# Narrower weights, skipped state products and a new order table in a gated-DeltaNet layer

## The chip, the cores and the metric

The kernel runs on one core of a Trainium2 chip. The metric is device time in microseconds (us). Before the change three runs gave 2718.79, 2718.13 and 2719.34 us, median 2718.79. All operands are float32; a matmul's operands can also be declared float32r, which the kernel uses for its large products by splitting every float into a high and a low part and adding three products.

## The reference, cut to what matters

One decoder layer (`DEPTH` is 1, so only layer 0) on 2048 tokens of width 1024. Its token mixer has eight gated-DeltaNet heads of width 128 and four heads that attend to a memory of 256 rows; their outputs go through one output projection, then a residual layer norm, an MLP with squared ReLU of width 4096, and a second layer norm. The part that the change touches is the chunked delta rule, with chunks of 64 rows in the reference:

```python
lower = jnp.where(strict, jnp.einsum('bnhcd,bnhsd->bnhcs', k_beta, kc) * decay, 0.0)
a_mat = jnp.eye(CHUNK, dtype=f32) + lower
u = lax.linalg.triangular_solve(a_mat, v_beta, left_side=True, lower=True, unit_diagonal=True)
w = lax.linalg.triangular_solve(a_mat, k_beta * jnp.exp(gc)[..., None], ...)
...
def step(state, inp):
    qd, kd, u_c, w_c, a_c, dc = inp
    v_new = u_c - jnp.einsum('bhcd,bhde->bhce', w_c, state)
    o = jnp.einsum('bhcd,bhde->bhce', qd, state) + jnp.einsum('bhcs,bhse->bhce', a_c, v_new)
    state = state * dc[..., None, None] + jnp.einsum('bhcd,bhce->bhde', kd, v_new)
    return state, o
s0 = jnp.zeros((B, H, Dk, v.shape[-1]), f32)
```

The first step starts from a zero state, and the state after the last step is not an output.

## The kernel before

**Tiling.** The tokens are taken in four blocks of 512 (`TB`), two blocks to a pair (`s` = 0, 1). In a block each head has four chunks of 128 rows (`NC`). A pair runs `mixer` for its two blocks (line 1655), then the output projection `out_seven` (line 1703), then `ff1` (1355) and `ff2` (1477). The last three are two-by-two block products that need seven block products instead of eight; in the profile their outputs are `ao`, `fA`, `fB`, `fC` and `f2A`, `f2B`, `f2C`. In `mixer` a step `t` runs `gdn_b` for head t-2, `gdn_a` for head t-1 and the projections of head t (`aq`, `ak`, `av`, and `az` for the gate), so that three heads are in work at once, and memory attention (`amq`, `sps`, `pmT`, `pmo`) stands between them.

**The inverse.** `invert` (line 889) inverts the unit lower triangular matrix of a head's four chunks. VectorE solves blocks of 16 rows; TensorE then doubles their size three times, each time by two products: `pq` (the off-diagonal block times the inverse so far) and `pp` (the inverse so far times `pq`). From 16 to 32 rows the weights are `LB` and `XB`, the latter with 112 columns. From 32 to 64 rows they are `L32` and `X32`, 128 columns wide, the two 32-row blocks of two chunks on the diagonal and 32 columns streamed through them (in the profile `pq<-Lq,inv` and `pp<-inv` with 128x32). From 64 to 128 rows they are `LP` and `X64` (`pq<-YP,inv` and `pp<-inv` with 128x64). Each `pq` and `pp` is two matmuls in float32, and there are 32 inversions (four blocks of eight heads). The tiles that hold these weights are zeroed once in a pair by `inverse_tiles` (line 551).

**The scan.** `gdn_b` (line 1074) walks the four chunks of a head: `pc<-state` and `po<-state` multiply k and the decayed q with the state, VectorE makes `R` from the first of them, `pc<-R,Y` applies the inverse, ScalarE copies the result to `vt`, `pc<-vt,kd` gives the state's increment, `po<-vt,at` completes the chunk's output, and VectorE updates the state. It does so for all 16 chunks, the first (zero state) and the last (state not read again) included. GpSimd sets the eight states to zero at the start (line 540).

**The end.** In `ff2` the last of the seven products adds, for eight groups of 512 rows of the weights (u = 0 to 7), into four banks, one for each tile of 128 tokens. Groups 0 to 4 go through the four tiles in turn. For the last three (`LT = 3`, line 1540) the order is turned round: tile 0 takes groups 5, 6 and 7, then tile 1, and so on, so that the tiles finish one after the other and each is normalized (`norm2`, DVE and GpSimd) and stored while TensorE does the next.

**What sets the order.** Each operation is first recorded (`Recorder.add`, line 225), with a cost by `cost` (line 277). `issue` (line 320) then runs a list scheduler over all of them: an operation becomes ready when its inputs' modelled ends are reached, plus a latency between the engines and `MARGIN` (100 ns, line 35), and of the ready ones each engine takes the one with the lowest priority number, which is its place in the program plus a shift from the table `PLACE` (line 190; keys such as `(0, 3, 'D')` name block, step and phase). The modelled starts give the order of every engine's instructions; on the chip each engine runs its own list in that order and waits where an operand is missing. All instructions are emitted at line 431, so a line number tells nothing; the names of the outputs do.

Of the kernel before, what the change touches and what calls it, by code (L numbers as in the profile page):

```python
# [11 lines left out]
ALU = mybir.AluOpType  # L12
# [22 lines left out]
MARGIN, TURN = 100, 40  # L35
# [149 lines left out]
class Op:  # L185
# [23 lines left out]
class Recorder:  # L209
# [110 lines left out]
    def issue(self):  # L320
# [50 lines left out]
        while True:  # L371
# [36 lines left out]
            for s in o.succ:  # L408
                lat = LAT.get((e, s.eng), LAT_FROM[e])
                if e == "PE" and lat and o.last < 60:  # L410
                    lat += 65 if o.last > 30 else 130
                if lat:
                    lat += MARGIN + (s.load if s.eng == "PE" and s.lhs in o.bufs else 0)
                s.ready = max(s.ready, o.end + (TURN if s.i in o.turns else lat))
                s.npred -= 1
                if s.npred == 0:
                    pending.append(s)
            for b in o.bufs:
                b.users -= 1
                b.end = max(b.end, o.end)  # L420
                if b.users == 0:
                    heapq.heappush(slots[b.key], b.end + LAT_FROM[e] + MARGIN)
                    again(b.key)
# [24 lines left out]
def hybrid_layer(  # L448
# [91 lines left out]
    for h in range(H):  # L540
        nc.gpsimd.memset(state[h], 0.0)
# [6 lines left out]
    INV = (("XB", (2, P)), ("LB", (2, P)), ("L32", (2, P)), ("X32", (2, P)), ("X64", (2, P)),  # L548
           ("LP", (2, P)), ("Q", (2 * P,)))

    def inverse_tiles():
        d = {}
        for i in range(0, len(INV), 2):
            t = slot("inv", "iv")
            nc.gpsimd.memset(t, 0.0)
            for j, (n, shape) in enumerate(INV[i:i + 2]):
                v = t[:, j * 2 * P:(j + 1) * 2 * P]
                d[n] = v if len(shape) == 1 else v.rearrange("p (u f) -> p u f", u=2)
        return d
# [184 lines left out]
    def gates(b, a):  # L744
# [46 lines left out]
        gc = G["gc"] = small("gc", sh, 2)  # L791
        gcf = gc.rearrange("p h c -> p (h c)")
        nc.vector.tensor_copy(gcf, pg[:, 0:32])
        G["ngc"] = small("ngc", sh, 2)
        nc.vector.tensor_scalar_mul(G["ngc"], gc, -1.0)
        kd = small("gkd", sh, 1)
# [15 lines left out]
        nc.tensor.transpose(pt[:32, :P], gcf, ident)  # L812
# [20 lines left out]
    def dense(b, h, T, G, w0=None):  # L833
# [29 lines left out]
        for n, nm in enumerate("kq"):  # L863
            pt = bank("pt" + nm, par)
            for c in range(NC):
                nc.tensor.transpose(pt[:, c * P:(c + 1) * P], res[nm][:, c * P:(c + 1) * P], ident)
            for c in range(NC):
                j = small("j" + nm, [P, P], 1)
                nc.scalar.activation(j, pt[:, c * P:(c + 1) * P], AF.Square,
                                     accum_out=ss[:, n * NC + c:n * NC + c + 1])  # L870
            if nm == "k":
                for c in range(NC):
                    nc.scalar.activation(kd[:, c * P:(c + 1) * P], pt[:, c * P:(c + 1) * P], AF.Copy,
                                         scale=G["ekd"][:, h, c:c + 1])
# [14 lines left out]
    def invert(L, par):  # L889
# [8 lines left out]
        for p in range(2):  # L898
            rows = slice(64 * p + 32, 64 * p + 64)
            nc.gpsimd.tensor_copy(L32[rows, :, 64 * p:64 * p + 32].part((0, p)), L[rows, 0:2, 64 * p:64 * p + 32])  # L900
            nc.vector.tensor_copy(L32[64 * p:64 * p + 32, :, 64 * p + 32:64 * p + 64].part((1, p)),
# [28 lines left out]
        XB, LB, X32, X64, Q = (inv[n] for n in ("XB", "LB", "X32", "X64", "Q"))  # L930
# [13 lines left out]
        Q16 = Q[:, :64].rearrange("p (u f) -> p u f", u=2)  # L944
# [4 lines left out]
        for c in range(2):  # L949
            nc.tensor.matmul(pp[:, c * 32:(c + 1) * 32], XB[:, c, :W], Q[:, c * 32:(c + 1) * 32].part(0, 3),  # L950
                             start=True, stop=True)
# [4 lines left out]
        ZP = Lq.rearrange("p c f -> p (c f)")[:, :64].rearrange("p (c f) -> p c f", c=2)  # L956
        Z = small("Z32", [P, NC, 32], 2)
        for p in range(2):
            odd = slice(64 * p + 32, 64 * p + 64)
            nc.vector.tensor_copy(ZP[64 * p:64 * p + 32].part(2 * p + 1), ZT[odd, 2:4])  # L960
            nc.scalar.copy(out=ZP[odd].part(2 * p), in_=ZT[odd, 0:2])
        nc.vector.transpose(Z.rearrange("p c f -> p (c f)"), ZT.rearrange("p c f -> p (c f)"))
        for p in range(2):
            for u in range(2):
                q = quads[2 * p + u]
                nc.vector.tensor_copy(X32[q, :, q].part((u, p)), Z[64 * p:64 * p + 32, 2 * u:2 * u + 2])
# [11 lines left out]
        pb = bank("pp", "ga%d" % par)[:, :64]  # L978
        pp = pb.rearrange("p (c f) -> p c f", c=2)
        for c in range(2):  # L980
            nc.tensor.matmul(pp[:, c], X32[:, c], Q[:, 64 + c * 32:64 + (c + 1) * 32].part(1), start=True, stop=True)
        Nf = Lq.rearrange("p c f -> p (c f)")[:, 64:]
        nc.scalar.activation(Nf, pb, AF.Copy, scale=-1.0)
        tr = Lq.rearrange("p c f -> p (c f)")[:64, :64]
        nc.vector.transpose(tr, Nf[:64])
        N3 = Nf.rearrange("p (c f) -> p c f", c=2)
        for p in (1, 0):
            o = Y3[64 * p:64 * p + 32, :, 64 * p + 32:64 * p + 64]
            nc.vector.tensor_copy(o[:, 2:4], N3[quads[2 * p + 1]])
            nc.scalar.copy(out=o[:, 0:2], in_=N3[quads[2 * p]])  # L990
        tr = tr.rearrange("p (c f) -> p c f", c=2)
        for u in range(2):
            nc.vector.tensor_copy(X64[quads[2 * u + 1], :, quads[2 * u]].part((u, 2)), tr[quads[u]])
# [7 lines left out]
        nc.scalar.copy(out=Q[:, P:].rearrange("p (c f) -> p c f", c=2).part(2), in_=pq)  # L1001
        pp = bank("pp", "ga%d" % par)[:, :P].rearrange("p (c f) -> p c f", c=2)
        for c in range(2):
            nc.tensor.matmul(pp[:, c], X64[:, c], Q[:, P + c * 64:P + (c + 1) * 64].part(2), start=True, stop=True)
# [12 lines left out]
    def gdn_a(h, r, G):  # L1017
# [50 lines left out]
        nc.scalar.activation(qd, gb, AF.Exp)  # L1068
        nc.vector.tensor_tensor(out=qd, in0=qd, in1=q, op=ALU.mult)
# [4 lines left out]
    def gdn_b(h, A, G, z, cat):  # L1074
# [5 lines left out]
        for c in range(NC):  # L1080
            pc = bank("pc", "pb")
            nc.tensor.matmul(pc[:, 0:P], k3[:, c], Sh, start=True, stop=True)
            nc.tensor.matmul(po[:, c], qd3[:, c], Sh, start=True, stop=False)
            R = small("R", [P, P], 2)
            nc.vector.scalar_tensor_tensor(out=R, in0=pc[:, 0:P], scalar=nbe[:, c:c + 1], in1=vb3[:, c],
                                           op0=ALU.mult, op1=ALU.add)
# [3 lines left out]
            nc.tensor.matmul(pc[:, 2 * P:3 * P], kd3[:, c], vt, start=True, stop=True)  # L1090
            nc.tensor.matmul(po[:, c], at3[:, c], vt, start=False, stop=True)
            nc.vector.scalar_tensor_tensor(out=Sh, in0=Sh, scalar=sc("el", c), in1=pc[:, 2 * P:3 * P],
                                           op0=ALU.mult, op1=ALU.add)
# [383 lines left out]
    def ff2(s, x1d):  # L1477
# [58 lines left out]
        for n, (xn, wn, bn, on, (th, nh)) in enumerate(SEVEN):  # L1536
# [3 lines left out]
            LT = 3 if last else 0  # L1540
# [114 lines left out]
    def mixer(b, T, w0, G):  # L1655
        i = b % 2
        r, A, z = {}, {}, {}
        for t in range(H + 2):
            spot(b, t, "B")
            if t >= 2:  # L1660
                c = cat_tile()
                gdn_b(t - 2, A.pop(t - 2), G, z.pop(t - 2), c[0])
                deliver(i, t - 2, *c)
            spot(b, t, "A")
            if 1 <= t <= H:
                A[t - 1] = gdn_a(t - 1, r.pop(t - 1), G)
# [250 lines left out]
```

## Time and profile before

| | |
|---|---|
| median of three runs | 2718.79 us |
| span of the profiled execution, first to last instruction | 2718.7 us |
| the profiled execution's own time | its span, which is 0.1 us from the median |
| TensorE (PE) busy, records | 2702.6 us (99%), 13625 |
| VectorE (DVE) busy | 2097.3 us (77%) |
| ScalarE (ACT) busy | 1627.0 us (60%) |
| GpSimd (POOL) busy | 403.6 us (15%) |
| mean granted TensorE clock | 0.999 |

In the views a group of instructions reads: line, engine, operation, output<-inputs, shape, count, then busy time of the group and mean duration of one, then the engine's idle time before them and what ended it. `128*112 128x32` at a matmul is weights of 128 rows and 112 columns with 32 columns streamed. A float32 matmul leaves two records, so 128 products of the scan leave 256; a transpose and a float32r matmul leave one. The ends of matmul records are modelled and overlap the next one's start, so what a matmul costs TensorE is read from the distance between starts, not from its duration. PEld is the weight load, which has a record of its own.

### The profile page before, as it was taken

To read this page: it belongs to the slowest core of one execution; us is meant where nothing else is said; L and a number is where in the kernel's file an instruction comes from. 1 tells how busy PE (TensorE), PEld (TensorE's weight loads), DVE (VectorE), ACT (ScalarE), POOL (GpSimd) and SP (SyncE) were. 2 spreads that over 40 slices of the span, in tenths; PEclk is the share of its full clock that TensorE was granted. 3 is DMA by queue.
4 is the path that set the end of the run, shared out by engine and by line. 5 is a ranking of instruction groups with operands and counts; after the bars stand their busy time and mean duration, and the time that the engine had idled before them with its cause. 6 is when DMAs were issued, how large, how long until landed. Compare 5 with 4: busy or idle time off the path is not lost.

```text
span 2718.7 us, 42521 instructions
## 1 busy us (share of the span) xinstructions
PE 2702.6 (99%) x13625; PEld 2264.0 (83%) x13625; DVE 2097.3 (77%) x5652; ACT 1627.0 (60%) x4106; POOL 403.6 (15%) x1031
## 2 busy tenths in 40 slices
PE   9999999999999999999999999999999999999998
PEld 7888888888888888888888888888888888888887
DVE  7999989998877776755767888788878666567575
ACT  7778767776575555334446776677656655554342
POOL 4233223331000000000022231332201000000000
PEclk9999999999999999999999999999999999999999
DMA  8766649867788888766663445444678644486673
GB/s 315 253 232 210 213 170 321 293 240 261 278 315 286 297 294 298 264 212 197 231 226 136 171 137 186 156 152 157 226 260 295 220 164 141 158 283 221 214 238 112
DMA packets 209072, 613.81 MB, mean 226 GB/s; under 512 B 24112, under 2 KB 32720, under 8 KB 188880
## 3 DMA queue, kind: packets, MB, share of 16 engines
q1 hardware_dynamic: 208416, 611.04, 64.7%
q8 instruction: 108, 1.77, 0.3%
q14 instruction: 116, 0.95, 0.1%
q10 hardware_dynamic: 432, 0.05, 0.0%
HBM read 436.35 MB, written 174.65 MB: 225 GB/s over the span
## 4 chain that ended last, share of the span: by engine, by line
PE 94%; DVE 2%; ACT 2%; DMA 1%; POOL 1%; issue 0%; SPq 0%; DVEq 0%; ACTq 0%; POOLq 0%
PE f2A L431 13%; PE fA L431 13%; PE ao L431 8%; PE fC L431 6%; PE f2C L431 6%; PE az L431 6%; PE aq L431 6%; PE av L431 6%; PE ak L431 6%; PE amq L431 3%; PE fB L431 3%; PE f2B L431 3%; PE pc L431 3%; PE po L431 2%; PE pkq L431 2%; PE pq L431 1%
## 5 line engine op out<-in xcount | busy, mean ns | idle before, releaser
L431 DVE TENSOR_TENSOR whl<-wraw,whl 128x512 fp32r<-128x512 f32 (+2 forms) x294 | 256.5, 883 | 109.8 <-ACT whl L431 107.9
L431 ACT CAST whl<-wraw 128x512 fp32r<-128x512 f32 (+2 forms) x294 | 226.4, 781 | 164.4 <-PE fC L431 54.5
L431 PE MATMUL fA<-B,whl 128*128 128x512 f32 x1152 | 279.1, 389 | 0.0
L431 PE MATMUL f2A<-whl,X 128*128 128x512 f32 x1152 | 262.1, 389 | 0.0
L431 ACT CAST X<-X 128x1024 fp32r<-128x1024 f32 x118 | 124.0, 1052 | 223.3 <-DMA X<-xsc 183.3
L431 PEld LDWEIGHTS fA<-B,whl 128*128 128x128 f32 x1152 | 216.2, 188 | 45.1
L431 PEld LDWEIGHTS f2A<-whl,X 128*128 128x128 f32 x1152 | 216.2, 188 | 44.9
L431 DVE TENSOR_TENSOR X<-X,X 128x1024 fp32r<-128x1024 f32 x118 | 143.8, 1221 | 126.0 <-ACT X L431 125.9
L431 PE MATMUL az<-T,whl 128*128 128x512 f32 x768 | 218.5, 406 | 0.0
L431 PE MATMUL aq<-T,whl 128*128 128x512 f32 x768 | 215.6, 406 | 1.7 <-DVE whl L431 0.8
L431 PE MATMUL ak<-T,whl 128*128 128x512 f32 x768 | 214.8, 407 | 0.1
L431 PE MATMUL av<-T,whl 128*128 128x512 f32 x768 | 209.1, 402 | 0.0
L431 PE MATMUL fC<-B,whl 128*128 128x512 f32 x768 | 192.3, 389 | 0.0
L431 PE MATMUL f2C<-whl,X 128*128 128x512 f32 x768 | 174.7, 389 | 0.0
L431 PEld LDWEIGHTS fC<-B,whl 128*128 128x128 f32 x768 | 144.1, 188 | 30.0
L431 PEld LDWEIGHTS f2C<-whl,X 128*128 128x128 f32 x768 | 144.1, 188 | 29.9
L431 PEld LDWEIGHTS aq<-T,whl 128*128 128x128 f32 x768 | 137.5, 189 | 27.4 <-DVE T L431 2.0
L431 PEld LDWEIGHTS av<-T,whl 128*128 128x128 f32 x768 | 138.5, 189 | 24.3
L431 PEld LDWEIGHTS ak<-T,whl 128*128 128x128 f32 x768 | 135.8, 189 | 22.3 <-ACT whl L431 0.4
L431 PEld LDWEIGHTS az<-T,whl 128*128 128x128 f32 x768 | 136.4, 189 | 21.2
L431 POOL TENSOR_SCALAR ve<-mv 128x1 f32<-128x1 f32 x34 | 15.3, 451 | 912.2 <-DVE mv L431 906.0
L431 PE MATMUL ao<-whl,X 128*128 128x512 f32 x528 | 136.8, 401 | 0.0
(294 smaller groups left out, 6292.2 us busy)
## 6 DMA issues: line engine op xcount, KB each, us to landing
whl<-wsc SPq DMA_DIRECT2D x108, 1024.0 KB, 4.9
wraw<-in_w_ff_dram SPq DMA_DIRECT2D x106, 512.0 KB, 4.3
X<-xsc SPq DMA_DIRECT2D x96, 512.0 KB, 4.1
wsc<-whl SPq DMA_DIRECT2D x36, 1024.0 KB, 6.4
whl<-tsc SPq DMA_DIRECT2D x64, 512.0 KB, 4.8
xsc<-hB SPq DMA_DIRECT2D x96, 256.0 KB, 2.5
xo<-cat SPq DMA_DIRECT2D x80, 256.0 KB, 4.1
wraw<-in_w_in_dram SPq DMA_DIRECT2D x35, 512.0 KB, 6.5
```

The source lines that it names most:

```text
L431: o.fn(*[res(a) for a in o.args], **{k: res(v) for k, v in o.kw.items()})
```

## The change

**Weights of 72 columns.** `L32` and `X32` become 72 columns wide (`W64`); the blocks of the two row pairs now stand side by side in 64 columns, and the streamed operands `Z64` and `Q64`, zero outside their blocks, are 64 columns wide for each of the two matmuls. So the pairs are `72x64` where they were `128x32`. ScalarE now copies `pq` with two copies of 64 partitions (before one of 128), and one transpose of 32 rows, one VectorE copy and one ScalarE copy stand where a transpose of 64 rows and two copies on each engine stood. The zeroed tiles are divided anew, still four.

**No products with the zero state.** In block 0 the first chunk has neither `pc<-state` nor `po<-state`; the inverse is applied to `vb` directly (`pc<-vb,Y`), and the state is copied from the increment. In block 3 the last chunk has no `pc<-vt,kd` and no update. The eight memsets of the states, a quarter of `qd` in block 0 and a quarter of `kd` in block 3 go too.

**Four last row groups by token tile.** `LT` is 4 in the last pair, so groups 4 to 7 of the last product go tile by tile.

**Slack behind GpSimd, and the order table.** `MARGIN` is now by engine, 400 ns behind GpSimd and 100 behind the others. `PLACE` has about twice as many entries, nearly all of them new. Beside these, the transpose `pgt` of the gates takes 96 columns in place of 32, of which 32 are used as before.

```diff
-MARGIN, TURN = 100, 40
+MARGIN, TURN = {"PE": 100, "DVE": 100, "ACT": 100, "POOL": 400, "SP": 100}, 40
...
-    ('w',): 140, (0, 0, 'H'): -305, (0, 1, 'D'): -225, (0, 1, 'H'): -435, (0, 1, 'Y'): -145, (0, 1, 'Z'): -165,
+    ('w',): 140, (0, 0, 'D'): 5, (0, 0, 'F'): -5, (0, 0, 'H'): -585, (0, 1, 'D'): -70, (0, 1, 'F'): 75,
...
-    for h in range(H):
-        nc.gpsimd.memset(state[h], 0.0)
...
-    INV = (("XB", (2, P)), ("LB", (2, P)), ("L32", (2, P)), ("X32", (2, P)), ("X64", (2, P)),
-           ("LP", (2, P)), ("Q", (2 * P,)))
+    W64 = 72
+    INV = ((("XB", (2, P)), ("LB", (2, P))), (("X64", (2, P)), ("LP", (2, P))),
+           (("L32", (2, W64)), ("X32", (2, W64)), ("Z64", (2, 64))),
+           (("Q64", (2, 64)), ("Q16", (64,)), ("N", (NC, 32)), ("Q", (P,))))
...
-        nc.tensor.transpose(pt[:32, :P], gcf, ident)
+        nc.tensor.transpose(pt[:96, :P], g3.rearrange("p j h c -> p (j h c)"), ident)
...
-        pq = bank("pq", "ga%d" % par)[:, :64].rearrange("p (c f) -> p c f", c=2)
+        pq = bank("pq", "ga%d" % par)[:W64, :P].rearrange("p (c f) -> p c f", c=2)
         for c in range(2):
             nc.tensor.matmul(pq[:, c], L32[:, c], ZP[:, c].part(0, 1, 2, 3), start=True, stop=True)
-        nc.scalar.copy(out=Q[:, 64:P].rearrange("p (c f) -> p c f", c=2).part(1), in_=pq)
...
+        for u in range(2):
+            nc.scalar.copy(out=QP[64 * u:64 * u + 64, :, 32 * u:32 * u + 32].part(u), in_=pq[:64, :, 32 * u:32 * u + 32])
+        pp = bank("pp", "ga%d" % par)[:W64, :P]
         for c in range(2):
-            nc.tensor.matmul(pp[:, c], X32[:, c], Q[:, 64 + c * 32:64 + (c + 1) * 32].part(1), start=True, stop=True)
...
+            nc.tensor.matmul(pp[:, c * 64:(c + 1) * 64], X32[:, c], QP[:, c].part(0, 1), start=True, stop=True)
...
+            begun, more = b > 0 or c > 0, b < NB - 1 or c < NC - 1
+            R = vb3[:, c]
+            if begun:
+                nc.tensor.matmul(pc[:, 0:P], k3[:, c], Sh, start=True, stop=True)
+                nc.tensor.matmul(po[:, c], qd3[:, c], Sh, start=True, stop=False)
...
+            if more:
+                nc.tensor.matmul(pc[:, 2 * P:3 * P], kd3[:, c], vt, start=True, stop=True)
+            nc.tensor.matmul(po[:, c], at3[:, c], vt, start=not begun, stop=True)
...
-            LT = 3 if last else 0
+            LT = (4 if 2 * s + 2 >= NB else 3) if last else 0
```

Three places show how the instructions move. The first is TensorE at the first inversion of block 0, the step from 32 to 64 rows; `az` and `amk` are products of the gate and of the memory's keys that fill the time between. Before:

```order
L431 MATMUL pp<-inv 112x32 x2
L431 MATMUL az<-T_192,whl 128x512
L431 MATMUL az<-T_218,whl 128x512
L431 MATMUL az<-T_225,whl 128x512
L431 MATMUL az<-T_218,whl 128x512 x2
L431 MATMUL az<-T_225,whl 128x512
L431 MATMUL pq<-Lq,inv 128x32 x2
L431 MATMUL az<-T_218,whl 128x512
L431 MATMUL az<-T_233,whl 128x512
L431 MATMUL az<-T_238,whl 128x512
L431 MATMUL az<-T_233,whl 128x512 x2
L431 MATMUL pp<-inv 128x32 x2
```

And after the change:

```order
L447 MATMUL pp<-inv 112x32 x2
L447 MATMUL av<-T_217,whl 128x512
L447 MATMUL amk<-mT,whl 128x256 x16
L447 MATMUL pq<-inv 72x64 x2
L447 MATMUL amk<-mT,whl 128x256 x8
L447 MATMUL az<-T_157,whl 128x512
L447 MATMUL az<-T_162,whl 128x512
L447 MATMUL az<-T_157,whl 128x512
L447 MATMUL pp<-inv 72x64 x2
```

The two pairs have 72 columns of weights and 64 streamed ones, and between them stand eight matmuls of 256 columns and three of 512 where five of 512 stood.

The second place is TensorE in block 0, where head 0's scan began beside the transposes of the memory rows (`pt<-ident,ym`). Before:

```order
L431 MATMUL pt<-ident,ym 128x128 x2
L431 MATMUL ptq<-ident,cq 128x128 x4
L431 MATMUL pt<-ident,ym 128x128 x8
L431 MATMUL pc<-state,ck 128x128
L431 MATMUL pt<-ident,ym 128x128 x4
L431 MATMUL aq<-T_171,whl 128x512
```

And after:

```order
L447 MATMUL az<-T_217,whl 128x512
L447 MATMUL pt<-ident,ym 128x128 x4
L447 MATMUL ptq<-ident,cq 128x128 x4
L447 MATMUL pt<-ident,ym 128x128 x12
L447 MATMUL aq<-T_157,whl 128x512
```

The product with the zero state is gone, and the last twelve transposes of the memory rows now follow each other.

The third place is VectorE at the kernel's end, from the third token tile's normalization on (`f2A` is the last product's bank, `mv` and `rs` the mean and the reciprocal deviation, `l2kq` the gain and the bias). Before:

```order
L431 BN_AGGR mv<-bn 128x2
L431 SCALAR_TENSOR_TENSOR y<-y,mv,l2kq_27882 128x512
L431 SCALAR_TENSOR_TENSOR y<-y,f2A 128x512
L431 SCALAR_TENSOR_TENSOR y<-y,mv,l2kq_27882 128x512
L431 BN_STATS bn<-y 128x6
L431 SCALAR_TENSOR_TENSOR y<-y,rs,l2kq_27917 128x512
L431 BN_AGGR mv<-bn 128x2
L431 SCALAR_TENSOR_TENSOR y<-y,rs,l2kq_27917 128x512
L431 SCALAR_TENSOR_TENSOR y<-y,mv,l2kq_27882 128x512 x2
L431 SCALAR_TENSOR_TENSOR y<-y,rs,l2kq_27917 128x512 x2
```

And after:

```order
L447 BN_AGGR mv<-bn 128x2
L447 SCALAR_TENSOR_TENSOR y<-y,mv,l2kq_27778 128x512 x2
L447 SCALAR_TENSOR_TENSOR y<-y,rs,l2kq_27813 128x512 x2
L447 SCALAR_TENSOR_TENSOR y<-y,f2A 128x512
L447 BN_STATS bn<-y 128x6
L447 BN_AGGR mv<-bn 128x2
L447 SCALAR_TENSOR_TENSOR y<-y,mv,l2kq_27778 128x512 x2
L447 SCALAR_TENSOR_TENSOR y<-y,rs,l2kq_27813 128x512 x2
```

The third tile's last three operations stand ahead of the last tile's addition, where they were mixed into the last tile's own work.

More of the change, by code (lines that the diff above doesn't have):

```diff
@@ L412, in issue @@
                 if lat:
-                    lat += MARGIN + (s.load if s.eng == "PE" and s.lhs in o.bufs else 0)
+                    lat += MARGIN[e] + (s.load if s.eng == "PE" and s.lhs in o.bufs else 0)
                 s.ready = max(s.ready, o.end + (TURN if s.i in o.turns else lat))
@@ L871, in dense @@
             if nm == "k":
-                for c in range(NC):
+                for c in range(NC - (b == NB - 1)):
                     nc.scalar.activation(kd[:, c * P:(c + 1) * P], pt[:, c * P:(c + 1) * P], AF.Copy,
@@ L929, in invert @@
         nc.vector.transpose(ZT.rearrange("p c f -> p (c f)"), Z.rearrange("p c f -> p (c f)"))
-        XB, LB, X32, X64, Q = (inv[n] for n in ("XB", "LB", "X32", "X64", "Q"))
+        XB, LB, X32, X64, Q, ZP, QP, N3 = (inv[n] for n in ("XB", "LB", "X32", "X64", "Q", "Z64", "Q64", "N"))
+        NT = v4(Q)
         Y = slot("Y", "s0")
@@ L949, in invert @@
         for c in range(2):
-            nc.tensor.matmul(pp[:, c * 32:(c + 1) * 32], XB[:, c, :W], Q[:, c * 32:(c + 1) * 32].part(0, 3),
+            nc.tensor.matmul(pp[:, c * 32:(c + 1) * 32], XB[:, c, :W], Q16[:, c].part(0, 3),
                              start=True, stop=True)
@@ L959, in invert @@
             odd = slice(64 * p + 32, 64 * p + 64)
-            nc.vector.tensor_copy(ZP[64 * p:64 * p + 32].part(2 * p + 1), ZT[odd, 2:4])
-            nc.scalar.copy(out=ZP[odd].part(2 * p), in_=ZT[odd, 0:2])
+            nc.vector.tensor_copy(ZP[64 * p:64 * p + 32, :, 32:].part(2 * p + 1), ZT[odd, 2:4])
+            nc.scalar.copy(out=ZP[odd, :, :32].part(2 * p), in_=ZT[odd, 0:2])
         nc.vector.transpose(Z.rearrange("p c f -> p (c f)"), ZT.rearrange("p c f -> p (c f)"))
@@ L1000, in invert @@
             nc.tensor.matmul(pq[:, c], LP[:, c], YP[:, c], start=True, stop=True)
-        nc.scalar.copy(out=Q[:, P:].rearrange("p (c f) -> p c f", c=2).part(2), in_=pq)
+        nc.scalar.copy(out=Q.rearrange("p (c f) -> p c f", c=2), in_=pq)
         pp = bank("pp", "ga%d" % par)[:, :P].rearrange("p (c f) -> p c f", c=2)
         for c in range(2):
-            nc.tensor.matmul(pp[:, c], X64[:, c], Q[:, P + c * 64:P + (c + 1) * 64].part(2), start=True, stop=True)
+            nc.tensor.matmul(pp[:, c], X64[:, c], Q[:, c * 64:(c + 1) * 64], start=True, stop=True)
         nc.vector.tensor_scalar_mul(Y3[:64, 2:4, 64:], pp[64:], -1.0)
@@ L1081, in gdn_b @@
             pc = bank("pc", "pb")
[L1082 to L1086, printed above, removed]
+            begun, more = b > 0 or c > 0, b < NB - 1 or c < NC - 1
[3 more added lines that the diff above has]
+                nc.tensor.matmul(po[:, c], qd3[:, c], Sh, start=True, stop=False)
+                R = small("R", [P, P], 2)
+                nc.vector.scalar_tensor_tensor(out=R, in0=pc[:, 0:P], scalar=nbe[:, c:c + 1], in1=vb3[:, c],
+                                               op0=ALU.mult, op1=ALU.add)
             nc.tensor.matmul(pc[:, P:2 * P], Y3[:, c], R, start=True, stop=True)
@@ L1089, in gdn_b @@
             nc.scalar.copy(out=vt, in_=pc[:, P:2 * P])
[L1090 to L1093, printed above, removed]
+            if more:
+                nc.tensor.matmul(pc[:, 2 * P:3 * P], kd3[:, c], vt, start=True, stop=True)
+            nc.tensor.matmul(po[:, c], at3[:, c], vt, start=not begun, stop=True)
+            if more and begun:
+                nc.vector.scalar_tensor_tensor(out=Sh, in0=Sh, scalar=sc("el", c), in1=pc[:, 2 * P:3 * P],
+                                               op0=ALU.mult, op1=ALU.add)
+            elif more:
+                nc.vector.tensor_copy(Sh, pc[:, 2 * P:3 * P])
         oss = sumsq(po, "oss")
```

62 lines of the change are left out of this document (29 added, 33 removed), and 44 rows, old and new, of the table PLACE.

## The prediction

> **What bounds the kernel now.** I read the page first, then TensorE's waits, then its groups by shape, then the timeline where small products stand. The page's engine rows and its chain:
>
> ```profile
> PE 2702.6 (99%) x13625; PEld 2264.0 (83%) x13625; DVE 2097.3 (77%) x5652; ACT 1627.0 (60%) x4106; POOL 403.6 (15%) x1031
> PE 94%; DVE 2%; ACT 2%; DMA 1%; POOL 1%; issue 0%; SPq 0%; DVEq 0%; ACTq 0%; POOLq 0%
> ```
>
> TensorE is busy for 2702.6 of 2718.7 us and is 94% of the chain. So what leaves TensorE's instruction stream should leave the time, unless a wait takes its place. TensorE's waits have eleven rows, from 1.4 us down to 0.2 us; these are the two longest, the one that names GpSimd in the body of the kernel, and the last:
>
> ```profile
> PE pt L431 <- ACT st L431: 1.4, 2, 0.9
> PE warm L431 <- POOL mhalf L518: 1.2, 1, 1.2
> ...
> PE pq L431 <- POOL inv L431: 0.3, 1, 0.3
> ...
> PE pt L431 <- ACT y L431: 0.2, 1, 0.2
> ```
>
> All eleven together are 6.4 us. A better order can win no more than that, 5.2 without the 1.2 us before the first matmul; the rest has to come from shorter or fewer products and from the tail behind the last matmul.
>
> Next, what a product costs, from starts. First a large one, from its group; then a stretch with eight records of 128-column weights and two large ones in it:
>
> ```profile
> L431 PE MATMUL f2A<-whl,X 128*128 128x512 f32 x1152 | 262.1, 389 | 0.0
> ```
>
> ```profile
> 122.23 0.38 PE L431 MATMUL pc<-vt,kd 128*128 128x128 f32 x2
> 122.45 0.39 PE L431 MATMUL po<-vt,at 128*128 128x128 f32 x2
> 122.67 0.53 PE L431 MATMUL pq<-Lq,inv 128*128 128x32 f32 x4
> 123.04 0.71 PE L431 MATMUL aq<-T,whl 128*128 128x512 f32 x2
> 123.58 0.38 PE L431 MATMUL pc<-state,ck 128*128 128x128 f32 x2
> ```
>
> A large product takes 262.1 / 1152 = 0.2275 us. From 122.23 to 123.58 are 1.35 us, less 2 x 0.2275 leaves 0.895 for eight small records: 0.112 each. They cost the same with 128 streamed columns and with 32, so the streaming does not set it; the weights of the next record do, since they are all 128 columns. The loads of 112 and of 32 columns show that:
>
> ```profile
> L431 PEld LDWEIGHTS pq<-ZT,inv 128*128 128x128 f32 x128 | 18.8, 190 | 2.1
> L431 PEld LDWEIGHTS pp<-inv 128*112 128x112 f32 x128 | 16.7, 176 | 2.7 <-ACT inv L431 0.7
> L431 PEld LDWEIGHTS aab<-xj,abw 128*32 128x32 f32 x64 | 1.5, 108 | 3.1 <-issue 2.7 <-DVE Xc L431 0.4
> ```
>
> 16 columns fewer are 14 ns less in the load, 0.875 ns per column; 96 fewer are 82 less, 0.854 per column. The line is straight.
>
> **The change part by part.** *Weights of 72 columns.* A pair is four records. The first load lies under the large product ahead, so four loads show: of records two to four, and of the large product behind. Now 4 x 0.112 = 0.448 us. With 56 columns fewer, three of them shrink by 56 x 0.875 = 49 ns to 0.063, the fourth does not: 3 x 0.063 + 0.112 = 0.301, that is 0.147 less. There are 2 pairs in each of 32 inversions: 64 x 0.147 = 9.4 us less. Twice the streamed columns cost nothing while a record streams faster than 0.063; these rows have the 64-column case beside the 32-column one:
>
> ```profile
> 108.95 0.53 PE L431 MATMUL pq<-Lq,inv 128*128 128x32 f32 x4
> 109.31 1.40 PE L431 MATMUL az<-T,whl 128*128 128x512 f32 x5
> ...
> 114.08 0.56 PE L431 MATMUL pq<-YP,inv 128*128 128x64 f32 x4
> 114.45 0.48 PE L431 MATMUL amk<-mT,whl 128*128 128x256 f32 x2
> ```
>
> Four records take 0.36 us to the next start with 32 columns and 0.37 with 64, where the last record alone shows its streaming: about 0.03 and 0.04 us, both under 0.063. No row has 72 columns of weights. Bounds: the distance at 112 columns, 14 ns less, gives 3 x 0.014 x 64 = 2.7 us, and that at 32 columns, 82 ns less and then held up by the streaming at about 0.04, gives 3 x 0.072 x 64 = 13.8 us. I take 9.4, between the rows on their line; the lower end is a rival below. A rule speaks against narrower weights: the Trainium skill, page "TensorE: Matmul & The Clock Gate", section "Weight-path perf modes", has a fast weight load that applies to full 128-column weights only and not to float32. If it were in force here all the same, leaving 128 columns would forfeit it, this term would be nothing at best and the sum -6.0; the load rows speak against it, since 112 columns load faster than 128, in proportion.
>
> *No products with the zero state.* 8 heads x (2 + 1) products = 24, with two records each at 0.112: 0.224 us a product, 5.4 us. One of them is covered: the product at 54.51 stands ahead of a wait for ScalarE, which ends when it ends:
>
> ```profile
> 54.51 0.39 PE L431 MATMUL pc<-state,ck 128*128 128x128 f32 x2
> 55.79 0.66 PE L431 MATMUL pt<-ident,ym 128*128 128x128 f32 x4 [0.90 <-ACT st L431]
> ```
>
> So 23 x 0.224 = 5.2 us. The twelve transposes that now follow each other there need the same bank evacuations from ScalarE, and I leave the wait at its 0.90. The eight memsets on GpSimd, VectorE's `R` and state update in these chunks and the quarters of `qd` and `kd` are off TensorE's path: nothing.
>
> *The wide transpose of the gates.* Four transposes load 96 columns in place of 32: 64 x 0.875 = 56 ns each, +0.2 us.
>
> *Tail.* After the last matmul VectorE has this to do:
>
> ```profile
> 2709.21 0.39 PE L431 MATMUL f2A<-whl,xl 128*128 128x512 f32 x1
> ...
> 2709.63 0.69 DVE L431 SCALAR_TENSOR_TENSOR y<-y,f2A 128x512 f32<-128x512 f32 x1 [0.43 <-PE f2A L431]
> 2710.24 0.75 DVE L431 SCALAR_TENSOR_TENSOR y<-y,mv,l2kq 128x512 f32<-128x512 f32 x1
> 2710.90 0.69 DVE L431 BATCH_NORM_STATS2 bn<-y 128x6 f32<-128x512 f32 x1
> 2711.50 0.74 DVE L431 SCALAR_TENSOR_TENSOR y<-y,rs,l2kq 128x512 f32<-128x512 f32 x1
> ...
> 2712.28 0.70 DVE L431 SCALAR_TENSOR_TENSOR y<-y,rs,l2kq 128x512 f32<-128x512 f32 x1
> ...
> 2714.22 1.41 DVE L431 SCALAR_TENSOR_TENSOR y<-y,rs,l2kq 128x512 f32<-128x512 f32 x2
> ```
>
> The ones at 2710.24, 2711.50 and 2712.28 are still the third tile's; the last tile takes from 2709.63 to 2715.63, 6.00 us. The first tile, with nothing before it, went through the same steps like this:
>
> ```profile
> 2697.39 0.69 DVE L431 SCALAR_TENSOR_TENSOR y<-y,f2A 128x512 f32<-128x512 f32 x1 [7.21 <-PE f2A L431]
> ...
> 2701.02 1.40 DVE L431 SCALAR_TENSOR_TENSOR y<-y,rs,l2kq 128x512 f32<-128x512 f32 x2
> ```
>
> 5.03 us. With four groups to a tile, tiles end 24 x 0.2275 = 5.46 us apart (18 x 0.2275 = 4.10 before), longer than the 5.03, so the third tile is done when the last begins: 6.00 - 5.03 = 1.0 us less. The price to look at is group 7's weights: they need the buffer of group 3, which is freed when the tile order starts, and they are wanted three groups later, 18 x 0.2275 = 4.10 us. Cast and subtraction of such a buffer went like this at the same place before:
>
> ```profile
> 2687.87 1.05 ACT L431 CAST whl<-wraw 128x1024 fp32r<-128x1024 f32 x1 [4.38 <-PE f2A L431]
> 2688.96 1.23 DVE L431 TENSOR_TENSOR whl<-wraw,whl 128x1024 fp32r<-128x1024 f32 x1 [4.21 <-ACT whl L431]
> ```
>
> 2.3 us from the release, on engines that had been idle for over 4 us: it fits, nothing lost.
>
> *Slack and order table.* The larger slack makes TensorE take a product that hangs on GpSimd 0.3 us later in the plan. It can save the one 0.3 us wait above and adds none by itself, since other products fill the place; the planned order holds buffers longer for it. The table moves thousands of instructions; I take it at zero, between -5.2 (every wait gone) and +6.4 (twice as many).
>
> Sum: -9.4 - 5.2 + 0.2 - 1.0 = -15.4 us. From the profiled execution, 2718.7 and 0.1 from the median: 2718.8 - 15.4 = 2703.4 us.
>
> **The rivals.** *Short loads have a floor.* If a record cannot go below the 0.112 - 0.014 = 0.098 of 112 columns, the 9.4 are 2.7: 2703.4 + 6.7 = 2710.1 us; at worst nothing is gained, 2712.8, which I count here. For it: the 32-column loads belong to products that write separate quarters of a bank, so no row has a chain of short loads, each behind the one before. Against: nothing in the rows bends. The same page, section "Wait — 56ns, not 53.3ns?", gives about 62 ns of sequencer time per MATMUL in one decoding mode; by it the floor would be 62 ns, an estimate that leaves 63 standing.
>
> *VectorE takes over in the first two blocks.* The stretch and its columns (PE, PEld, DVE, ACT, POOL busy):
>
> ```profile
> 70.00:620.00 550.00, 548.26 (x3160) 467.93 (x3159) 502.80 (x1935) 411.47 (x1358) 168.86 (x418) 1.00 0.68 242
> ```
>
> VectorE is at 91%. If it allowed no shorter block, half of the 9.4 and 15 of the 23 products (3.4) would be lost: 2703.4 + 8.1 = 2711.5. Against: all of TensorE's waits together are 6.4 us, and the change takes a copy from VectorE in every inversion.
>
> *ScalarE between `pq` and `pp`, slower than before.* The second product waits for ScalarE's copy, now two:
>
> ```profile
> 109.72 0.21 ACT L431 COPY inv<-pq 128x64 f32<-128x64 f32 x1
> 109.96 1.05 ACT L431 CAST whl<-wraw 128x1024 fp32r<-128x1024 f32 x1
> ...
> 110.55 0.53 PE L431 MATMUL pp<-inv 128*128 128x32 f32 x4
> ```
>
> `pq` ends at 109.48, the copy starts 0.24 later and ends at 109.93, `pp` starts at 110.55: 0.62 later, of which 0.24 is the same hand-over, so 0.38 to spare. A second copy of 0.21 fits. With a cast of 1.05 in front of it, it is 1.05 + 0.21 - 0.38 = 0.88 late, and TensorE waits. In all 32 inversions that is 28 us: 2731.6. It decides from 15.4 / 0.88 = 18 inversions on. For it: casts stand all over ScalarE's list. Against: in 30 of 32 inversions the new list has the two copies behind each other, and more products between the pairs than before.
>
> *The order alone removes the waits*: 2703.4 - 5.2 = 2698.2.
>
> **How the numbers follow.** Forecast 0.70 (2703.4), waits gone 0.12 (2698.2), floor 0.08 (2710.1), VectorE 0.06 (2711.5), ScalarE 0.04 (2731.6). The range from 2698.0 to 2710.4 takes in the first three and leaves out 0.10 for the others; twice the waits would be 2709.8, inside it. What this kernel's measurement can tell from no change is about 0.2%, 5.4 us, so faster means below 2713.4: 0.70 + 0.12 + 0.08 and a third of the VectorE case make 0.92; the rest of that case and a quarter of ScalarE's make 0.05 the same; 0.03 slower.
>
> **What would show it.** Right: `pq` and `pp` with 128*72 have loads near 141 ns (190 - 49) and four records near 0.30 us with the exposed load behind; TensorE has 48 records fewer; the span behind the last matmul goes from 9.1 us (2718.7 - 2709.6) to about 8.1; TensorE's waits stay near 6 us. Wrong: records of 72 columns at 0.1 us or more; a row of TensorE's waits of several us with ScalarE or VectorE behind it; or a tail that is no shorter since group 7's weights come late.

## The result, and the profile after

After the change five runs gave 2702.22 to 2704.65 us, median 2702.39; five runs of the kernel before, taken between them, 2718.13 to 2719.61, median 2718.79. The ratio is 0.9943, with a 95% interval from 0.9933 to 0.9953. The forecast was 2703.4 in a range from 2698.0 to 2710.4. One of the eleven runs of e12 below took 4999 us at a granted clock of 0.54 and is left out of its figures.

The profiled execution of after took 2702.34 us, its span is 2700.6: the time is 1.7 longer than the span. The prediction had put before's span of 2718.7 equal to its time. If the same 1.7 holds there, that execution took 2720.4, above its median; so the spans differ by 18.1 us and the medians by 16.4. Here are the engine rows and the chain of after's page:

```profile
PE 2685.2 (99%) x13577; PEld 2248.5 (83%) x13577; DVE 2087.0 (77%) x5604; ACT 1624.8 (60%) x4098; POOL 423.3 (16%) x1023
PE 96%; DVE 2%; ACT 1%; DMA 0%; issue 0%; POOL 0%; POOLq 0%; ACTq 0%; DVEq 0%
```

TensorE has 48 records fewer and is now 96% of the chain. The short loads in the groups by shape, and then one pair in TensorE's timeline:

```profile
L447 PEld LDWEIGHTS pq<-inv 128*72 128x72 f32 x128 | 13.2, 143 | 3.4
```

```profile
129.23 0.76 PE L447 MATMUL pkq<-kq 128*128 128x256 f32 x5
129.83 0.41 PE L447 MATMUL pq<-inv 128*72 128x64 f32 x4
130.05 0.36 PE L447 MATMUL amk<-mT,whl 128*128 128x256 f32 x1
130.25 0.39 PE L447 MATMUL ak<-T,whl 128*128 128x512 f32 x1
```

A load takes 143 ns, forecast near 141. The four records take 0.22 us to the start of `amk`. That one takes 0.20 to the next start, where a record of 256 columns takes 0.60 / 5 = 0.12 in the row above, so 0.08 is the exposed load of 128 columns. 0.22 + 0.08 = 0.30, as forecast. Behind the last matmul stands:

```profile
2691.78 0.39 PE L447 MATMUL f2A<-whl,xl 128*128 128x512 f32 x1
2692.20 0.69 DVE L447 SCALAR_TENSOR_TENSOR y<-y,f2A 128x512 f32<-128x512 f32 x1 [0.46 <-PE f2A L447]
2692.93 0.69 DVE L447 BATCH_NORM_STATS2 bn<-y 128x6 f32<-128x512 f32 x1
...
2695.78 1.42 DVE L447 SCALAR_TENSOR_TENSOR y<-y,rs,l2kq 128x512 f32<-128x512 f32 x2 [0.46 <-POOL rs L447]
```

VectorE needs from 2692.20 to 2697.20, 5.00 us, where 5.03 was forecast, and nothing of the third tile is left in between (`...` marks rows that are left out here). From the last matmul's end to the span's end it is 2700.6 - 2692.2 = 8.4 us, 0.7 less than before's 9.1, since the store behind VectorE took 0.3 longer. TensorE's waits, the longest four of ten rows (6.6 us in all; before 6.4 in eleven):

```profile
PE ao L447 <- ACT whl L447: 1.4, 4, 0.6
PE warm L447 <- POOL mhalf L534: 1.2, 1, 1.2
PE pt L447 <- ACT st L447: 1.1, 1, 1.1
PE pt L447 <- ACT y L447: 1.0, 2, 0.9
```

### The profile page after: what moved, and what is told of

Read it like the earlier page. It is cut to its first block, busy times and chain, and to the rows that moved or that the text cites. A ratio compares the mean times of both kernels' runs of the same rounds, so it can differ in the third digit from the quotient of the medians.

```text
span 2700.6 us, 42393 instructions
## 1 busy us (share of the span) xinstructions
PE 2685.2 (99%) x13577; PEld 2248.5 (83%) x13577; DVE 2087.0 (77%) x5604; ACT 1624.8 (60%) x4098; POOL 423.3 (16%) x1023
## 4 chain that ended last, share of the span: by engine, by line
PE 96%; DVE 2%; ACT 1%; DMA 0%; issue 0%; POOL 0%; POOLq 0%; ACTq 0%; DVEq 0%
PE f2A L447 13%; PE fA L447 13%; PE ao L447 8%; PE az L447 7%; PE fC L447 6%; PE f2C L447 6%; PE av L447 6%; PE ak L447 6%; PE aq L447 6%; PE fB L447 3%; PE f2B L447 3%; PE amq L447 3%; PE pc L447 3%; PE po L447 2%; PE pkq L447 2%; PE pq L447 1%
## 5 line engine op out<-in xcount | busy, mean ns | idle before, releaser
L447 PE MATMUL fA<-B,whl 128*128 128x512 f32 x1152 | 286.4, 389 | 0.0
```

The lines of the kernel that those rows point to most:

```text
L447: o.fn(*[res(a) for a in o.args], **{k: res(v) for k, v in o.kw.items()})
```

## The experiments

Twelve kernels, five or eleven runs each. The ratio is to the kernel before on the same chip (its median was 2718.6 to 2718.8 each time); the kernel after was timed only in the five runs above. "Waits" is the sum of all rows of TensorE's waits in the profiled execution; "slow clock" is, in windows of 4 us ahead of the kernel's end, the sum of 4 us times what the granted clock lacked to 1. These two columns are of one execution each; e7's was 5.3 us above its kernel's median, e9's 2.7, e10's 2.5 and e3's 1.4.

| kernel | us, median | ratio, 95% | waits | slow clock |
|---|---|---|---|---|
| before | 2718.8 | 1 | 6.4 | 0 |
| after | 2702.4 | 0.9943 [0.9933, 0.9953] | 6.6 | 0 |
| e1, 96 columns | 2705.8 | 0.9951 [0.9938, 0.9965] | 6.7 | 0 |
| e2, 64 columns | 2717.0 | 0.9993 [0.9984, 1.0001] | 5.7 | 0 |
| e3, three last groups | 2705.3 | 0.9950 [0.9938, 0.9963] | 7.9 | 1.7 |
| e4, zero products back | 2718.6 | 1.0000 [0.9991, 1.0009] | 10.6 | 1.7 |
| e5, old table and slack | 2715.4 | 0.9990 [0.9981, 0.9999] | 11.7 | 1.7 |
| e6, new table and slack alone | 2731.9 | 1.0048 [1.0036, 1.0061] | 11.8 | 1.7 |
| e7, slack 100 | 2719.4 | 1.0002 [0.9993, 1.0011] | 16.1 | 5.1 |
| e8, 72 columns alone | 2739.2 | 1.0073 [1.0061, 1.0086] | 19.7 | 10.2 |
| e9, zero products, order held | 2714.0 | 0.9982 [0.9973, 0.9991] | 13.2 | 1.7 |
| e10, none, before's order held | 2716.3 | 0.9991 [0.9982, 1.0000] | 9.1 | 0 |
| e11, 66 columns | 2704.5 | 0.9945 [0.9931, 0.9959] | 6.7 | 1.7 |
| e12, four last groups alone | 2717.4 | 0.9996 [0.9987, 1.0005] | 6.3 | 0 |

**e1, e2 and e11: the columns.** The planner is told 72 in all three, so every instruction keeps its place:

```diff
-    W64 = 72
+    W64 = 96
...
+            mo = 72 if mo == 96 and n == 64 else mo
```

The second line is in `cost`; e2 has 64 and e11 66 in place of 96.

Expected of e1:

> The changed kernel with 96 columns for L32 and X32 in place of 72, every instruction in the same order. If the time is TensorE's stream and a record costs its successor's weight load, the pairs' records go from 0.063-0.065 us to about 0.085 and the time rises by 3 x 0.021 x 64 = 4.0 us, to about 2706.4. If the gain came from the new order, nothing moves: 2702.4.

Expected of e2:

> The changed kernel with 64 columns, every instruction in the same order. By the straight line of the loads: records of 0.056 us, 3 x 0.007 x 64 = 1.3 us less than 2702.4, about 2701.1. Rival: weights of 64 columns or fewer make TensorE change its mode for the pair and back, and it drains each time; at a record's modelled 0.17 us beyond its streaming twice in each of 64 pairs that is 22 us more, so anything from 2705 up speaks for it. The Trainium skill, page TensorEngine Tiling (Array Packing), section Tiling Modes, says that a change of tiling mode drains the engine.

Expected of e11:

> The kernel after with 66 columns in place of 72, the order held. By the line of spacing over columns (0.063 us at 72, so about 0.058 at 66) 64 x 4 x 0.005 = 1.3 us less than after: 2701.1 us within 1. Rival: the loss seen at 64 columns begins above 64 already: 2710 us or more.

The same pair as above, in TensorE's timelines of e1, e11 and e2:

```profile
130.46 0.47 PE L448 MATMUL pq<-inv 128*96 128x64 f32 x4
130.74 0.36 PE L448 MATMUL amk<-mT,whl 128*128 128x256 f32 x1
130.94 0.40 PE L448 MATMUL ak<-T,whl 128*128 128x512 f32 x1
```

```profile
130.32 0.40 PE L448 MATMUL pq<-inv 128*66 128x64 f32 x4
130.53 0.36 PE L448 MATMUL amk<-mT,whl 128*128 128x256 f32 x1
130.73 0.39 PE L448 MATMUL ak<-T,whl 128*128 128x512 f32 x1
```

```profile
129.57 0.64 PE L448 MATMUL pkq<-kq 128*128 128x256 f32 x4
130.14 0.45 PE L448 MATMUL pq<-inv 128*64 128x64 f32 x4
130.52 0.39 PE L448 MATMUL amk<-mT,whl 128*128 128x256 f32 x1
130.74 0.39 PE L448 MATMUL ak<-T,whl 128*128 128x512 f32 x1
```

From the first record of the pair to `ak` it is 0.48 us with 96 columns, 0.42 with 72, 0.41 with 66. 96 against 72 is 64 x 0.06 = 3.8 us; the medians differ by 3.4 and the line gave 4.0. All the pairs say the same: over their 256 records, the distances from each start to the next add up to 23.6 us in before (128 columns), 18.4 with 96, 14.5 with 72 and 13.6 with 66. The loads take 190, 163, 143 and 138 ns. So the line holds from 128 to 66, and the rival of a floor falls; with 66 columns four records take 0.21 us, 0.052 each, so there is none at 0.062 either.

With 64 columns it is 0.60, and the four `pkq` ahead take 0.57 to the pair's start where they take 4 x 0.12 = 0.48 in after. That is 0.27 us lost in this pair, with narrower weights; over all 64 the medians lose 14.6, 0.23 each. Both the step in and the step out of the pair got longer. The loss is in no load (136 ns at 64 columns) and in no listed wait (5.7 us in all, 6.6 in after). The Trainium skill, page "TensorEngine Tiling (Array Packing)", section "Available Configurations", lists 128 rows by 64 columns as a tiling of its own, and its section "Key Properties" says that changing the mode drains TensorE; these rows agree with that, though no run shows that the mode is the cause. The loss starts between 66 and 64. 66 columns are worth 64 x 0.01 = 0.6 us by these rows, 0.9 by the sum; e11's runs (2702.28 to 2704.89, median 2.1 above after's) don't show it.

**e3 and e12: the tail.** e3 puts the change back to three groups, e12 puts four into the kernel before. All instructions ahead of the last groups keep their order.

```diff
-            LT = (4 if 2 * s + 2 >= NB else 3) if last else 0
+            LT = 3 if last else 0
```

Expected of e3:

> The changed kernel with three last row groups by token tile. The last tile's work on VectorE goes back from 5.00 to 6.00 us behind the last matmul: 1.0 us more than 2702.4, 2703.4; at least 0.7, the difference that the two spans show behind the last matmul (9.1 and 8.4). Rival: the last transfer hides it, no difference.

Expected of e12:

> The kernel before with four last row groups by token tile; only VectorE's last instructions change place. Theory of the tail: VectorE's work behind the last matmul falls from 6.0 to 5.0 us, so 1.0 us less, 2717.7 us within 1. Rival by e3, which was 2.9 us slower than after with three groups: 2715.9 us or less.

VectorE's first and last rows behind the last matmul, in e3 and in e12:

```profile
2695.86 0.69 DVE L447 SCALAR_TENSOR_TENSOR y<-y,f2A 128x512 f32<-128x512 f32 x1 [0.43 <-PE f2A L447]
...
2700.44 1.41 DVE L447 SCALAR_TENSOR_TENSOR y<-y,rs,l2kq 128x512 f32<-128x512 f32 x2
```

```profile
2707.51 0.69 DVE L431 SCALAR_TENSOR_TENSOR y<-y,f2A 128x512 f32<-128x512 f32 x1 [0.46 <-PE f2A L431]
...
2711.08 1.41 DVE L431 SCALAR_TENSOR_TENSOR y<-y,rs,l2kq 128x512 f32<-128x512 f32 x2 [0.46 <-POOL rs L431]
```

5.99 us with three groups, 4.98 with four: the term is 1.0. e12 was 1.2 faster than before, which its interval can't tell from nothing. e3 was 2.9 slower than after, more than its tail explains. Its profiled execution (2706.7) shows 1.7 more in the middle of the kernel, in the same instructions. First the granted clock (fourth figure) in windows of after, then of e3, where the same products stand 2 us later (1.4 of these were already lost by 311 us, in a stretch where the two kernels have the same order, so they are not the edit's):

```profile
2064.00:2066.00 2.00, 1.78 (x7) 1.00 1.02 399
2066.00:2068.00 2.00, 2.00 (x13) 1.00 1.07 395
2068.00:2070.00 2.00, 2.00 (x12) 1.00 1.05 363
```

```profile
2066.00:2068.00 2.00, 1.78 (x5) 0.71 0.84 310
2068.00:2070.00 2.00, 2.00 (x6) 0.50 1.05 387
2070.00:2072.00 2.00, 2.00 (x12) 0.94 1.14 374
```

e3's clock is halved for 3.4 us there ((0.29 + 0.50 + 0.06) x 2 / 0.5), and the products take twice as long: 1.7 us lost. What stands ahead in TensorE's timeline of e3:

```profile
2064.26 0.55 PE L447 MATMUL pt<-ident,y 128*128 128x128 f32 x3 [0.88 <-ACT y L447]
2064.97 0.55 PE L447 MATMUL pt<-ident,y 128*128 128x128 f32 x3 [0.16 <-ACT y L447]
2065.90 0.73 PE L447 MATMUL ao<-whl,xh 128*128 128x512 f32 x2 [0.39 <-ACT whl L447]
2066.85 1.65 PE L447 MATMUL ao<-whl,xh 128*128 128x512 f32 x3 [0.22 <-ACT whl L447]
```

After has the same four waits, 0.88, 0.16, 0.39 and 0.22, and kept its clock. e11 lost it at the same place.

**e4: the products with the zero state and the unread increments put back**, planned anew.

```diff
-            begun, more = b > 0 or c > 0, b < NB - 1 or c < NC - 1
+            begun, more = True, True
```

> The changed kernel with the products with the zero state, the last state's product and update, and the full qd and kd put back. Stream theory: 24 x 0.224 = 5.4 us more on TensorE, 5.2 if one of them stands under a wait: about 2707.6. Rival: the planner fits them into waits of the new order, less than 2 us: under 2704.4.

Measured: 16.2 us slower than after, so both theories missed. The waits grew by 4.0 us and one stretch of slow clock (1.7) was added; with the products' 5.4 that makes 11.1, and 5 stay unassigned. The planner had moved more than 1,600 of TensorE's 13,577 records (compared in the two traces), though the table was the same: it takes what is ready, and with 24 products more other things are ready at a given moment. That made the order a suspect, which the forecast had taken at zero.

**e5 to e8: which table with which program.** e5 is after with before's `PLACE` and slack; e6 is before with after's; e7 is after with only this edit; e8 has the 72 columns with their copies alone, the rest as before but for the gates' wide transpose. The edit of e7:

```diff
-MARGIN, TURN = {"PE": 100, "DVE": 100, "ACT": 100, "POOL": 400, "SP": 100}, 40
+MARGIN, TURN = {"PE": 100, "DVE": 100, "ACT": 100, "POOL": 100, "SP": 100}, 40
```

Expected of e5:

> The changed program (72 columns, no products with the zero state, four last row groups) with the order table and the slack of before. Theory A, the order is worth nothing and the time is that of TensorE's stream of records: 2702.4 us, within 3 us. Theory B, a table suits only the program that it goes with, and with any other program small waits return: 2707 us or more, up to about 2718, with the waits spread over the heads and the stream's own records unchanged. Theory C, the new table and slack are a better order in themselves: 2707 us or more too, and then the old program gains by the new table.

Expected of e6:

> The program of before with the new order table and the new slack behind GpSimd alone. Theory A (the order is worth nothing): 2718.8 us, within 3 us. Theory B (a table suits only its own program): 2724 us or more. Theory C (the new order is better in itself): 2713 us or less.

Expected of e7:

> The kernel after with the slack behind GpSimd at 100 as for the other engines, and the new table kept. Theory A: 2702.4 us, within 2 us. Theory B: the planner counts other ready times behind GpSimd's results, so the order differs from the one that the table was made with: 2704 to 2714 us. Theory C: 2705 us or more, and then the waits that return are behind GpSimd.

Expected of e8:

> The 72-column weights alone: the products with the zero state are back, three last row groups, the table and slack of before. Theory A (64 pairs by 0.147 us shorter, nothing else): 2709.4 us, within 2 us. Theory B: the records are 9.4 us shorter, but the table was made with another inverse, so 5 us or more come back as small waits: 2714 to 2724 us, with 4 records of a pair still at 0.063 us each.

All four are slower than the same program with its own table and slack, by 13.0 (e5, from after), 13.2 (e6, from before), 17.0 (e7, from after) and 20.5 us (e8, from before). Theory A falls everywhere. Theory C falls with e6: the new table and slack make the old program slower. In e7 it falls too: the one row of its waits that names GpSimd is the 1.2 us before the first matmul, as in after. Theory B stands, though it set e7 and e8 too low. The longest waits of e8, with the weights and inputs of the output projection (`ao`) late:

```profile
PE ao L431 <- DVE whl L431: 3.5, 3, 1.8
PE ao L431 <- ACT whl L431: 2.7, 3, 1.8
PE ao L431 <- ACT X L431: 2.0, 1, 2.0
```

And the granted clock around one of them, in windows of e8:

```profile
680.00:684.00 4.00, 3.37 (x19) 1.00 0.59 206
684.00:688.00 4.00, 2.16 (x8) 0.70 0.35 121
688.00:692.00 4.00, 4.00 (x11) 0.50 0.02 6
692.00:696.00 4.00, 4.00 (x20) 0.95 0.03 11
```

A mismatched order pays twice: for the wait (1.84 us from 684.55 on), and for the clock that falls with it (it lacks 3.4 us here, 10.2 in the whole of e8). The columns' 9.4 off, 13.3 more of waits and 10.2 of slow clock are 14.1 more than before; 20.5 were measured. Of e5's 13.0 us, waits and slow clock make 6.8. A part of the rest lies in what a wait counts: it begins at the modelled end of the record ahead, and a large product's record lasts 0.39 us where the next can start after 0.23, so the first 0.16 us of each stall are in no wait. e8 has 22 more waits than before: 3.5 us, an estimate. What is left (some 3 us of e8, more of e5) stays unassigned.

**e9 and e10: the zero products with the order held.** In e9 the planner doesn't know of 24 added products, which `rec.put` hangs on the instruction recorded next; their results are not used. In e10 it plans before's program, and an instruction with an empty `rec.put` is then not issued; VectorE copies `vb` where it added nothing to it.

```diff
+            if not begun:
+                rec.put = [(pc[:, 0:P], k3[:, c], R), (pc[:, 2 * P:3 * P], k3[:, c], R)]
...
+            if not more:
+                rec.put = [(pc[:, 2 * P:3 * P], k3[:, c], vt)]
```

```diff
+            rec.put = None if begun else ()
             nc.tensor.matmul(pc[:, 0:P], k3[:, c], Sh, start=True, stop=True)
```

Expected of e9:

> The kernel after, with 24 products of 128 columns by 128 rows issued again next to where the dropped ones stood (in the first block two behind each first product with the inverse, in the last block one behind each last product with the state's values); their results are not used, and every other instruction keeps the place that it has in the kernel after. Theory B (the products cost their records, and the rest of what e4 lost came from its new order): 24 x 0.224 = 5.4 us more than after, 2707.8 us within 1.5. Rival: the products themselves cost what e4 lost, 2714 us or more. Second rival: they fall into waits, 2704 us or less.

Expected of e10:

> The kernel before with its order held and the 24 products with the zero state and into the state that nobody reads left out, VectorE copying the values in place of the step that added nothing to them. Theory B: 2718.75 - 5.4 = 2713.4 us within 1.5, and TensorE's waits grow by less than 1 us. Rival: the removed records leave gaps, since what stands behind them was waiting for VectorE and ScalarE anyway: 2717 us or more.

e9 was 11.6 slower than after, which by its number is the rival's case. What the products cost by themselves shows in the first block. The place of the first two in TensorE's timeline of after and of e9:

```profile
115.01 0.49 PE L447 MATMUL pc<-vb,Y 128*128 128x128 f32 x2
115.26 0.71 PE L447 MATMUL aq<-T,whl 128*128 128x512 f32 x2
```

```profile
115.58 0.49 PE L448 MATMUL pc<-vb,Y 128*128 128x128 f32 x2
115.91 0.61 PE L450 MATMUL pc<-vb,ck 128*128 128x128 f32 x4
116.27 0.71 PE L448 MATMUL aq<-T,whl 128*128 128x512 f32 x2
```

(L450 is the line of the added products.) From `pc<-vb,Y` to `aq` it is 0.25 us in after and 0.69 in e9: 0.44 for two products, 0.22 each. The same instruction near the block's end, in after and e9:

```profile
507.81 1.43 PE L447 MATMUL ak<-T,whl 128*128 128x512 f32 x5 [0.49 <-ACT cq L447]
```

```profile
511.78 1.43 PE L448 MATMUL ak<-T,whl 128*128 128x512 f32 x5 [0.49 <-ACT cq L448]
```

16 products stand ahead of it: 16 x 0.224 = 3.6 us, and it starts 3.97 later. This agrees, but loosely: in e3, with no product added, it starts at 509.31, 1.50 later than in after.

The last block's eight products cost far more, by a fault of this edit. They read k, whose buffer VectorE wants next. VectorE's wait in e9, its place, what TensorE then waits for, and the clock:

```profile
DVE cz L448 <- PE pc L450: 4.5, 2, 2.3
```

```profile
1842.49 0.69 DVE L448 SCALAR_TENSOR_TENSOR cz<-th,az 128x512 f32<-128x512 f32 x1 [2.21 <-PE pc L450]
...
1846.92 0.44 PE L448 MATMUL pp<-inv 128*72 128x64 f32 x4 [2.17 <-DVE inv L448]
```

```profile
1848.00:1852.00 4.00, 4.00 (x12) 0.57 0.65 223
```

They kept a buffer 2.2 us longer, VectorE stood, TensorE ran dry, and its clock fell. So e9's 11.6 are not the price of 24 products; the 0.22 each in the first block can be read. The sum agrees: the profiled execution's span is 14.4 us longer than after's (2715.0 against 2700.6), and 5.4 for the products, 6.6 more of waits and 1.7 of slow clock make 13.7.

e10 gained 2.3 us instead of 5.4, between theory B and the rival; the interval reaches from 0 to 4.9. In its profiled execution, 2.5 us above its own median, the waits are 2.7 us longer than in before, where less than 1 was expected. The longest is one that before has not:

```profile
109.35 0.58 PE L433 MATMUL pp<-inv 128*112 128x32 f32 x4 [1.93 <-ACT inv L433]
```

ScalarE was late because its cast ahead waited 1.9 us longer for a load of weights than in before and started 2.3 us later. The cast in ScalarE's timeline of e10 and of before:

```profile
106.50 1.05 ACT L433 CAST whl<-wraw 128x1024 fp32r<-128x1024 f32 x1 [6.36 <-DMA wraw<-in_w_mem_k_dram]
```

```profile
104.23 1.05 ACT L431 CAST whl<-wraw 128x1024 fp32r<-128x1024 f32 x1 [4.46 <-DMA wraw<-in_w_mem_k_dram]
```

Whether the usual execution of e10 loses its 3 us in that way isn't shown, so where the other half of the 5.4 went stays open.

## Why the prediction was right

*72 columns, -9.4.* Right in mechanism and size: loads of 143 ns, pairs of 0.30 us, 9.1 us less over all the pairs' records, and the way back to 96 columns costs what the line says. The tie of spacing and load breaks at 64, which the forecast had not looked at; that the change stops at 72 was the kernel's choice and not the forecast's merit: with the 64 columns that the blocks need, the whole change would have gained 1.8 us (2717.0 against 2718.8).

*No zero products, -5.2.* Right for the pair of program and table that was timed: 48 records fewer, and 0.22 us per product in e9's first block. As a gain in time by itself it is less firm: e10 found 2.3 us of it in the old order.

*Tail, -1.0.* Right on VectorE: 6.00 to 5.00 us in after, and 4.98 in e12. Behind the last matmul 0.7 of it was left in after (8.4 us, where 8.1 was forecast), since the store took 0.3 longer. Group 7's weights were in time: the last product shows no wait.

*The wide transpose of the gates, +0.2.* No run tests it.

*Slack and order table, 0, between -5.2 and +6.4.* The value came out right, the reason only half: waits went from 6.4 to 6.6 us, but not since the order matters little. With another table or slack the same records took 13 to 17 us more (e5 to e7), outside the bounds that I gave, since I bounded the term by the waits of before and not by those that a new plan can make. As far as e5 and e8 show, the other edits could gain their sum only with the table that came with them: 72 columns alone, worth -9.4 in records, made the kernel 20.5 us slower.

*The sum.* -15.4 forecast, -16.4 measured. The further 1.0 is less than the spread of single runs (2702.22 to 2704.65 here).

*The rivals.* A floor for short loads: against it 0.30 us a pair, and 0.052 a record with 66 columns. A price for leaving 128 columns: the loads get shorter at every step down. VectorE as the bound in the first two blocks, and ScalarE between `pq` and `pp`: no row of TensorE's waits in after is over 1.4 us, and products added to the first block cost their full price there. The order alone removing waits: after still has 6.6 us of them, and e6 has 11.8.

## What to carry to other kernels

On a kernel that one engine bounds at 99%, cost an edit by that engine's spacing between starts; here that part held. Then ask what plan the edit will run under: where a scheduler's table goes with one program, as here, no edit can be judged with the old table, and none of its parts alone; hold the order and change the size of an instruction to measure it. When weights get narrower, time the widths next to the one that the data needs: here 64 columns were slower than 66, 72 and 96.

## What the runs showed of the hardware

A group of four records with 64 columns of weights, between records of 128, costs about 0.23 us more than one with 72: the records drift apart on both sides of it (0.57 us in place of 0.48 ahead, 0.60 in place of 0.42 from the first on).

TensorE's clock halves after short gaps. In eight of the fourteen profiled executions it was granted at half in the midst of work, 13 times in all, for 3.4 us or twice that; each 3.4 us cost 1.7. In the 4 us ahead of each, TensorE had stood idle for 1.4 to 2.3 us, in one wait or several: in e9 one of 2.17, in e3 four that add up to 1.65 within 3.5 us. A wait of 1.93 in e10, and the four of 1.65 in after, left it whole. Where one execution has several stretches, they begin at whole multiples of 3.4133 us from each other: in e7 after 195 and 397 of them (665.60 and 1355.09 us).

The Trainium skill, page "TensorE: Matmul & The Clock Gate", section "What's actually happening", has a window of 3413 ns that runs freely and a clock that halves after one idle window; the length and the multiples agree with that, but the gaps here were about half a window long. The runs of after lie at 2702.2 to 2702.4 and at 2704.0 to 2704.7; one such stretch in some of them would do that, but only one of the five was profiled, and the mean clock on record, 0.999 in four of them and 0.998 in the run of 2704.00, is too coarse to tell.
